# Unread products in TensorE's waits and one operation for a token selection's one-hots, in a diffusion layer with expert choice

## The chip, the cores and the metric

The kernel runs on one core of one Trainium2 chip. The metric is the device time of one execution in microseconds, taken as the median over several runs. The engines are TensorE (PE in the profile; its weight loads are listed apart as PEld), VectorE (DVE), ScalarE (ACT), GpSimd (POOL) and SyncE (SP), which here only issues DMAs.

## The reference

One layer of a diffusion backbone on 1024 latent tokens of 1024 features and 256 context tokens: a mixer (differential attention and a gated linear recurrence side by side, one output projection), and then a mixture of experts in which each expert chooses its tokens. The change touches the second part and the way into it:

```python
def expert_choice_ffn(h, w_router, w_gate, w_up, w_down):
    b_, t_, d_ = h.shape
    cap = CAPACITY_FACTOR * t_ // N_EXPERTS        # 2 * 1024 // 16 = 128
    aff = softmax(einsum("btd,de->bte", h, w_router))
    top_aff, top_idx = top_k(swapaxes(aff, 1, 2), cap)
    xin = h[top_idx]                               # 128 tokens for each expert
    g = einsum("becd,edf->becf", xin, w_gate)
    u = einsum("becd,edf->becf", xin, w_up)
    y = einsum("becf,efd->becd", silu(g) * u, w_down) * top_aff
    return zeros.at[top_idx].add(y)
```

Sixteen experts each take the 128 tokens with the highest affinity to them, run a gated feed-forward of width 1024 on these, and add the weighted result to the tokens' rows.

## The kernel before

**Router tail (lines 1338 to 1363).** The last tiles of the output projection are followed by the router's three steps for tiles 5, 6 and 7: `route_a` (norm and transposition), `route_b` (affinities), `route_c` (the stream that is gathered later, stored to DRAM as `h2d`). This is one chain over DVE, GpSimd (a power), ACT and PE.

**Search (lines 1422 to 1453).** The 128th highest affinity of each of the 16 experts is found by bits in ten rounds, for all experts at once. A round adds seven steps to the best value so far (`cand`, L1442), compares all affinities with the candidates in two halves (`reach`, shown as T, L1447), counts over the tokens with eight products against a matrix of ones (`tot`, L1450), and keeps the highest candidate that at least 128 tokens reach (`best`, L1452 and L1453). Between the products and `best` a generator, `spare()`, gives DVE one operation of other work in some rounds. In round 4 pools change and the next weights are asked for.

**Slots (L1457 to L1470).** From the thresholds each token gets its slot 1 to 128 in each expert's list, by sums over tokens: 24 small products into `sl_ps`.

**A token selection, `pick(e)` (L1477) and `gather(e)` (L1486).** For each of the eight tiles of 128 tokens DVE compares an iota row with the tile's slots (L1482), which gives a 128x128 one-hot matrix, and PE multiplies it, as the stationary operand, with a table of five columns (`aux`: affinity in three parts and two parts of the token's number) into `ix` (L1483). `gather` copies that (L1491), makes the index (L1492), and starts an indirect DMA of 128 rows into `xg` (L1498). The rows are transposed in two groups of four (`tr`, L1504), and split in a high part (`xhi`, ACT, L1505) and a low part (`xlo`, DVE, L1506).

**The experts (L1516 to L1664).** Every weight comes in pieces of 512 KB, 24 for an expert, through a ring of `AHEAD` = 37 places that SyncE's queue fills. A piece is split in a high part (`mhi`, ACT, L1380) and a low part (`mlo`, DVE, L1381), three buffers of each, and each product of the reference is three of PE's: high by high, high by low, low by high (L1525 to L1527 for gate and up, L1614 to L1616 for down).

**What sets the order.** Up to L1644 PE, DVE and ACT work in the order that is written. Behind it, until the last expert, the framework's scheduler sets the order of each engine; it may also put work from behind that line ahead of what is written in front of it. DMAs on SyncE's queue go in order.

```python
    pick(0)
    gather(0)
    for i in range(LEAD):
        make()
    pick(1)
    ms.__exit__(None, None, None)
    tk_st.close()
    x_T(0, 0)
    x_T(0, 1)
    gather(1)
```

Of the kernel before, what the change touches and what calls it, by code (L numbers as in the profile page):

```python
# [32 lines left out]
def shape_constants():  # L33
    """Tables that depend on shapes alone."""
    c = {}
    c["k_ident"] = np.eye(128, dtype=np.float32)
    i = np.arange(64)
    m = [((i[:, None] // (2 * h) == i[None, :] // (2 * h)) & (i[:, None] // h != i[None, :] // h)) for h in LEVELS[:-1]]
    c["k_masks"] = np.tile(np.stack(m, 1).astype(np.float32).reshape(64, -1), (2, 1))
    i = np.arange(128)  # L40
    half = 32
    inv = (1.0 / (np.float32(10000.0) ** (np.arange(0, half, 2, dtype=np.float32) / np.float32(half)))).astype(np.float32)
    t = np.arange(T)
    ang_r = ((t // 64).astype(np.float32)[:, None] * inv).astype(np.float32)
    ang_c = ((t % 64).astype(np.float32)[:, None] * inv).astype(np.float32)
    ang = np.concatenate([ang_r, ang_r, ang_c, ang_c], -1)
    sign = np.where((np.arange(64) % 32) < 16, -1.0, 1.0).astype(np.float32)
    c["k_cos"] = np.ascontiguousarray(np.tile(np.cos(ang).T, (2, 1)))
    c["k_sin"] = np.ascontiguousarray(np.tile((np.sin(ang) * sign).T, (2, 1)))
    c["k_tri"] = (i[:, None] <= i[None, :]).astype(np.float32)  # L50
    c["k_iota"] = np.tile(np.arange(1, 129, dtype=np.float32), (128, 1))
    c["k_pos"] = np.stack([np.tile(np.arange(8, dtype=np.float32), (128, 1)),
                           np.tile(i[:, None].astype(np.float32), (1, 8))], -1).reshape(128, 16)
    step = np.arange(1, 8)[None, :] << np.arange(12, -1, -3)[:, None]
    c["k_step"] = np.tile(step.reshape(-1).astype(np.float32), (128, 1))
    return c


def weave(main, back):
    """Emit two lists of steps in proportion, the second filling in between the steps of the first."""  # L60
    n, m = len(main), len(back)
    j = 0
    for i, f in enumerate(main):
        f()
        while j < m and (j + 1) * n <= (i + 1) * m:
            back[j]()
            j += 1
    while j < m:
        back[j]()
        j += 1  # L70
# [3 lines left out]
def layer(ctx: ExitStack, tc, a, out):  # L74
# [28 lines left out]
    def rstd_of(dst, ss, n, w):  # L103
        """dst = (ss / n + eps) ** -0.5 on [128, w]"""
        nc.vector.tensor_scalar(dst, ss, 1.0 / n, EPS, op0=OP.mult, op1=OP.add)
        nc.gpsimd.tensor_tensor(dst, dst, half_neg[:, :w], op=OP.pow)
# [4 lines left out]
    def cut(halves, ts, hs=slice(None)):  # L111
        """heads hs, tokens ts of a transposed output kept in two halves of the tokens"""
        b, t0 = divmod(ts.start, 512)
        return halves[b][:, hs, t0:t0 + ts.stop - ts.start]
# [44 lines left out]
    def unit_T(job, ppool, t0, n):  # L159
        """transposed output [cols, tokens t0..t0+n]"""  # L160
        def f():
            pp = ppool.tile([128, 512], F32, name="pp", bufs=2)
            for k in range(KT):
                whi, wlo = job.piece(job.hi, k), job.piece(job.lo, k)
                hh, hl = h_hi[t0 // 512][:, k, :], h_lo[t0 // 512][:, k, :]
                nc.tensor.matmul(pp[:, :n], whi, hh, start=(k == 0), stop=False)  # L166
                nc.tensor.matmul(pp[:, :n], whi, hl, start=False, stop=False)  # L167
                nc.tensor.matmul(pp[:, :n], wlo, hh, start=False, stop=(k == KT - 1))  # L168
            job.evac(pp, t0, n)
        return f  # L170

    def unit_N(job, ppool, t, halves=False):
        """natural output, two token tiles t, t + 1, 256 columns"""
# [96 lines left out]
    def hgrn_steps(h):  # L270
# [23 lines left out]
        def blocks(lhs, rhs):  # L294
            """the products of 64 x 64 blocks, half z of tile t on the partitions from 64 z"""
# [231 lines left out]
    # shift and scale: each of their four blocks of 512 columns has its own columns of the array  # L527
# [22 lines left out]
    def small_vectors():  # L550
        nc.vector.tensor_copy(masks.rearrange("p l s -> p (l s)"), mf[:, :masks.shape[1] * 64])
        # small vectors as columns
# [76 lines left out]
    def trans_pair(p):  # L629
        """token tiles 2p, 2p + 1 transposed"""  # L630
# [7 lines left out]
    def mod_pair(p):  # L638
        """modulated, split"""
# [48 lines left out]
    for h in range(4):  # L688
        if h < 3:
            weave(phases[h + 1], hgrn_steps(h))  # L690
        else:
            # the gates multiply finished heads only: head 3's gate waits for its recurrence
# [34 lines left out]
    # the rest of adaLN: rows of gate 1, shift 2, scale 2, gate 2  # L727
# [62 lines left out]
    def prep_first():  # L790
        """the scaled queries and the keys of head 0 as hi and lo, stacked along the contraction for each map"""
# [24 lines left out]
    def prep_steps(h):  # L816
        """the same for a later head, in steps: (for the scalar engine, for the vector engine and the queue)"""
# [152 lines left out]
    def early_weights():  # L970
        """the keys and queries are all stacked: their place goes to the first weights of the output projection"""
# [35 lines left out]
    def mm_y(y, oh, ol, k, n):  # L1007
        """one product of the output projection; oh, ol: the block of k of the activations"""
# [17 lines left out]
    def split_da(hs):  # L1026
        """heads hs of the first two tiles of tokens"""
# [12 lines left out]
    def rest_weights():  # L1040
        """in the order of the places of the raw weights: those of oyd come free first"""
# [17 lines left out]
    # router on the normed stream: the modulation goes into its weights and into a bias  # L1059
# [118 lines left out]
    # A piece is 128 rows of each partition's share: of the gate or of the projection up (half of the columns, two  # L1178
    # blocks of the contraction) or of the projection down (one block).
    AHEAD, LEAD, MAN = 37, 2, 1  # L1180
# [5 lines left out]
    def ring():  # L1186
        """the next place of the ring"""
# [37 lines left out]
    def prep(i):  # L1225
        """the residual, and the activations of the output projection as hi and lo"""
# [52 lines left out]
    def route_b(i, tag="o"):  # L1279
        """the affinities; each fourth of the contraction on its own columns of the array, the fourths then summed"""  # L1280
# [26 lines left out]
    def route_c(i, n=None, queue=nc.sync):  # L1307
        """the modulated stream, to be gathered; in two steps"""
# [46 lines left out]
    next(close7)  # L1355
    next(route6)
    run(route_b(5))
    next(close7)
    run(route_b(6, "atr"))
    run(route_c(6))  # L1360
    run(route_a(7, True))
    run(route_b(7))
    rw, rw_st = pool("rw", side="right")

# [11 lines left out]
    def split_piece(u):  # L1376
        """a fetched piece as hi and lo"""
# [13 lines left out]
    def spare():  # L1391
        """what the vector engine does while the tensor engine counts"""
# [19 lines left out]
    # The 128th highest value of each expert, three bits of it at a time: first the upper 15 of its 30 bits, then  # L1412
    # the lower ones, with every value that the upper ones put above (below) at the upper (lower) end. In 16 bits.
# [6 lines left out]
    for r in range(10):  # L1420
        if r == 4:
# [4 lines left out]
            # what the first expert needs lies where the last tile of tokens is still at work, the ring above it  # L1426
# [22 lines left out]
        for i in range(8):  # L1449
            nc.tensor.matmul(tot, onesb, reach[:, :, i, :], start=(i == 0), stop=(i == 7))  # L1450
        next(todo, None)
        nc.vector.scalar_tensor_tensor(b0[:, 1:8, :], tot, CAP - 0.5, cand, op0=OP.is_ge, op1=OP.mult)  # L1452
        nc.vector.tensor_reduce(b1[:, 0, :], b0.rearrange("p j e -> p e j"), axis=AX.X, op=OP.max)  # L1453
    # slots 1..128 in token order, higher values before those equal to the 128th
# [20 lines left out]
    mops, mops_st = pool("mops", space=PSUM)  # L1475

    def pick(e):  # L1477
        x = ex[e]
        ix = mops.tile([128, 8], F32, name="ix")
        for i in range(8):  # L1480
            oh = mo.tile([128, 128], BF, name="onehot", bufs=3)
            nc.vector.tensor_scalar(oh, iota, slot[:, 0, i, e:e + 1], None, op0=OP.is_equal)  # L1482
            nc.tensor.matmul(ix[:, 0:5], oh, aux[:, i, e, :], start=(i == 0), stop=(i == 7))  # L1483
        x.ix = ix

# [55 lines left out]
    # Every row is closed with what the experts before the last gave it; then the rows of the last one anew.  # L1541
# [90 lines left out]
    def take(u):  # L1632
        """a piece of the weights; the pieces after it are split ahead of their use"""
# [5 lines left out]
    pick(0)  # L1639
    gather(0)  # L1640
    for i in range(LEAD):
        make()
    pick(1)
# [5 lines left out]
    for e in range(NE):  # L1649
        if e == NE - MAN:  # L1650
            ms = tc.manual_schedule(engines={nc.tensor.engine, nc.vector.engine, nc.scalar.engine, nc.gpsimd.engine})
            ms.__enter__()
        gate_up(e, 0)
        if e + 2 < NE:
            pick(e + 2)
# [43 lines left out]
```

## Time and profile before

| | |
|---|---|
| median of 3 runs | 1558.53 us (1556.73 to 1561.23) |
| span of the profiled execution | 1557.5 us |
| its median-to-span difference | 1.0 us |
| PE busy | 1447.3 us (93%) |
| PEld busy | 1191.3 us (76%) |
| DVE busy | 1166.5 us (75%) |
| ACT busy | 875.7 us (56%) |
| POOL busy | 115.4 us (7%) |

An engine's busy time is the sum of its instructions without overlap; PEld runs beside PE. In the span's chain of waits PE stands for 37% and no other engine for more than 2%, the rest being in shorter steps. A time in the rows below is in us from the start of the span. What follows is read from stretches of the span, since the shares over the whole mix stages with different limits: the router tail, the search and the first selection lie between 886 and 976 us, the later experts behind it.

### The profile page before, as it was taken

The page shows a single profiled execution, that of the slowest core. Times are in us where ns is not written, and L with a number is a line of the kernel's source. Part 1 is how long each engine was busy: PE and PEld are TensorE (multiplying, and loading weights), DVE is VectorE, ACT ScalarE, POOL GpSimd, SP SyncE. Part 2 cuts the span into 40 slices and gives each one's busy share as a digit, 9 for nine tenths or more (in the row PEclk, how much of TensorE's full clock was granted, in tenths as well). Part 3 has the DMA queues.
Part 4 walks back from the last instruction along what each step waited for, and adds up shares of the span by engine and source line. Part 5 has one row for each costly group of instructions (what it writes and reads, how often), then busy time and mean ns, then how long its engine had stood idle before and what let it go on. Part 6 is the DMA issues. An engine that isn't in the chain of part 4 may idle for free. (4 is left out here: it accounts for less than half of the span.)

```text
span 1557.5 us, 23415 instructions
## 1 busy us (share of the span) xinstructions
PE 1447.3 (93%) x8808; PEld 1191.3 (76%) x8808; DVE 1166.5 (75%) x1700; ACT 875.7 (56%) x1350; POOL 115.4 (7%) x139
## 2 busy tenths in 40 slices
PE   6999999999999988999999839999999999999990
PEld 1888988888977777999878627777777777777770
DVE  2627472849177769999845578999999999999983
ACT  1734443444211127889843406787777787877781
POOL 1100000000000001110000000110000000000003
PEclk9899999999999998999999859999999999999995
DMA  9210110011166526434056887999999999999736
GB/s 335 82 54 29 28 28 28 29 41 29 30 194 180 177 56 156 96 84 134 15 173 219 303 292 267 365 373 383 365 376 385 378 384 384 367 383 380 270 122 148
DMA packets 159309, 316.28 MB, mean 203 GB/s; under 512 B 13790, under 2 KB 50870, under 8 KB 159196
## 3 DMA queue, kind: packets, MB, share of 16 engines
q1 hardware_dynamic: 148592, 277.99, 50.0%
q0 software_dynamic: 9408, 33.54, 9.1%
q10 hardware_dynamic: 1196, 3.26, 0.6%
q8 instruction: 69, 1.13, 0.3%
q14 instruction: 44, 0.36, 0.1%
HBM read 274.36 MB, written 29.38 MB: 195 GB/s over the span
## 5 line engine op out<-in xcount | busy, mean ns | idle before, releaser
L1381 DVE TENSOR_TENSOR mlo<-mraw,mhi 128x1024 fp32r<-128x1024 f32 x340 | 406.0, 1220 | 25.0 <-ACT mhi L1380 22.1
L1380 ACT CAST mhi<-mraw 128x1024 fp32r<-128x1024 f32 x340 | 354.9, 1051 | 100.2 <-PE g L1526 44.3
L166 PE MATMUL pp<-h_hi,whi 128*128 128x512 f32 (+1 forms) x480 | 180.1, 375 | 0.0
L167 PE MATMUL pp<-h_lo,whi 128*128 128x512 f32 (+1 forms) x480 | 178.4, 372 | 0.0
L168 PE MATMUL pp<-h_hi,wlo 128*128 128x512 f32 (+1 forms) x480 | 178.1, 371 | 0.0
L150 ACT CAST whi<-wraw 128x512 fp32r<-128x512 f32 x64 | 39.6, 621 | 121.5 <-PE pp L167 59.6
L1525 PE MATMUL g<-mhi,xhi 128*128 128x512 f32 x256 | 106.5, 416 | 0.7 <-ACT xhi L1505 0.7
L1614 PE MATMUL my<-mhi,hhi 128*128 128x512 f32 x256 | 104.3, 407 | 0.0
L881 DVE TENSOR_REDUCE sm<-s 128x1 f32<-128x1280 f32 x64 | 95.2, 1490 | 12.0 <-PE s L876 9.6
L166 PEld LDWEIGHTS pp<-h_hi,whi 128*128 128x128 f32 x480 | 90.5, 189 | 17.6 <-ACT T L478 0.9
L168 PEld LDWEIGHTS pp<-h_hi,wlo 128*128 128x128 f32 x480 | 90.5, 188 | 17.0 <-issue 1.7
L1527 PE MATMUL g<-mlo,xhi 128*128 128x512 f32 x256 | 103.1, 403 | 0.2
L1616 PE MATMUL my<-mlo,hhi 128*128 128x512 f32 x256 | 103.1, 403 | 0.1
L1526 PE MATMUL u<-mhi,xlo 128*128 128x512 f32 x256 | 102.5, 400 | 0.0
L167 PEld LDWEIGHTS pp<-h_lo,whi 128*128 128x128 f32 x480 | 90.5, 189 | 15.6 <-issue 0.9
L1527 PE MATMUL u<-mlo,xhi 128*128 128x512 f32 x256 | 102.2, 399 | 0.0
L1615 PE MATMUL my<-mhi,hlo 128*128 128x512 f32 x256 | 101.6, 397 | 0.0
L1525 PE MATMUL u<-mhi,xhi 128*128 128x512 f32 x256 | 101.5, 396 | 0.0
L1526 PE MATMUL g<-mhi,xlo 128*128 128x512 f32 x256 | 101.3, 396 | 0.0
L185 PE MATMUL pp<-whi,h_hi 128*128 128x256 f32 x320 | 93.3, 291 | 2.0 <-ACT h_hi L651 2.0
L343 DVE TENSOR_TENSOR X<-X,T 128x640 f32<-128x640 f32 (+1 forms) x112 | 78.2, 759 | 20.4 <-ACT KM L321 12.8
L186 PE MATMUL pp<-whi,h_lo 128*128 128x256 f32 x320 | 92.1, 288 | 0.7 <-DVE h_lo L652 0.7
(323 smaller groups left out, 3135.3 us busy)
## 6 DMA issues: line engine op xcount, KB each, us to landing
mraw<-in_w_gate_dram SPq DMA_DIRECT2D x114, 512.0 KB
mraw<-in_w_up_dram SPq DMA_DIRECT2D x113, 512.0 KB
mraw<-in_w_down_dram SPq DMA_DIRECT2D x113, 512.0 KB
wraw<-in_w_in_dram SPq DMA_DIRECT2D x32, 512.0 KB
aw<-in_w_ada_dram SPq DMA_DIRECT2D x64, 256.0 KB
aw<-in_w_ada_dram SPq DMA_DIRECT2D x16, 512.0 KB
T<-in_w_up_dram SPq DMA_DIRECT2D x15, 512.0 KB
T<-in_w_down_dram SPq DMA_DIRECT2D x15, 512.0 KB
```

The costliest lines, as they stand in the source:

```text
L166: nc.tensor.matmul(pp[:, :n], whi, hh, start=(k == 0), stop=False)
L167: nc.tensor.matmul(pp[:, :n], whi, hl, start=False, stop=False)
L168: nc.tensor.matmul(pp[:, :n], wlo, hh, start=False, stop=(k == KT - 1))
L881: nc.vector.tensor_reduce(self.sm[:, m:m + 1], s, axis=AX.X, op=OP.max, negate=True)
L1380: nc.scalar.copy(hi, r)
L1381: nc.vector.tensor_sub(lo, r, hi)
L1525: nc.tensor.matmul(o, x.hi[:, k, :], hi[:, kk, :], start=(k == 0), stop=False)
L1526: nc.tensor.matmul(o, x.lo[:, k, :], hi[:, kk, :], start=False, stop=False)
L1527: nc.tensor.matmul(o, x.hi[:, k, :], lo[:, kk, :], start=False, stop=(k == 7))
L1614: nc.tensor.matmul(y[:, ns], x.hh[:, k, :], hi[:, ns], start=(k == 0), stop=False)
L1615: nc.tensor.matmul(y[:, ns], x.hl[:, k, :], hi[:, ns], start=False, stop=False)
L1616: nc.tensor.matmul(y[:, ns], x.hh[:, k, :], lo[:, ns], start=False, stop=(k == 7))
```

## The change

`keep_on(o, n)` is new: it issues n bf16 products of 128x128 by 128x512, of the matrix of ones with itself repeated, into a part of PSUM that nothing reads. They are put between the steps of the router tail (3, 4, 3 and 3, and 9 behind it), behind the counting products of each round (5, and 8 in round 4), behind the first `gather` (8) and behind the second `pick` (14): 97 in all. `pick` makes its eight one-hots with one DVE operation over 128x1024 into one buffer (before: eight operations, three buffers), and returns a function that issues the eight products, which for the later experts is called between the two halves of the gate and up projection. The ring has 36 places instead of 37. The rest of the diff takes comments out.

```diff
-    AHEAD, LEAD, MAN = 37, 2, 1
+    AHEAD, LEAD, MAN = 36, 2, 1
...
+    def keep_on(o, n):
+
+        for _ in range(n):
+            nc.tensor.matmul(o, onesb, onesb[:, None, :].to_broadcast([128, 4, 128]), start=True, stop=True)
+    idle = atps.tile([128, TA], F32, name="s1")[:, 0:512]
     next(route6)
     run(route_b(5))
+    keep_on(idle, 3)
     next(close7)
     run(route_b(6, "atr"))
     run(route_c(6))
-    run(route_a(7, True))
-    run(route_b(7))
+    keep_on(idle, 4)
+    route7 = route_a(7, True)
+    next(route7)
+    keep_on(idle, 3)
+    next(route7)
+    rb = route_b(7)
+    next(rb)
+    keep_on(idle, 3)
+    run(rb)
+    keep_on(idle, 9)
...
             nc.tensor.matmul(tot, onesb, reach[:, :, i, :], start=(i == 0), stop=(i == 7))
+        keep_on(idle, 8 if r == 4 else 5)
         next(todo, None)
...
         ix = mops.tile([128, 8], F32, name="ix")
-        for i in range(8):
-            oh = mo.tile([128, 128], BF, name="onehot", bufs=3)
-            nc.vector.tensor_scalar(oh, iota, slot[:, 0, i, e:e + 1], None, op0=OP.is_equal)
-            nc.tensor.matmul(ix[:, 0:5], oh, aux[:, i, e, :], start=(i == 0), stop=(i == 7))
+        oh = mo.tile([128, 8, 128], BF, name="onehot")
+        nc.vector.tensor_tensor(oh, iota[:, None, :].to_broadcast([128, 8, 128]),
+                                slot[:, 0, :, e:e + 1].to_broadcast([128, 8, 128]), op=OP.is_equal)
+
+        def counts():
+            for i in range(8):
+                nc.tensor.matmul(ix[:, 0:5], oh[:, i, :], aux[:, i, e, :], start=(i == 0), stop=(i == 7))
         x.ix = ix
+        return counts
...
-    pick(0)
+    pick(0)()
     gather(0)
+    idle = mops.tile([128, 512], F32, name="g", bufs=2)
+    keep_on(idle, 8)
     for i in range(LEAD):
         make()
-    pick(1)
+    pick(1)()
+    keep_on(idle, 14)
     ms.__exit__(None, None, None)
...
+        counts = pick(e + 2) if e + 2 < NE else None
         gate_up(e, 0)
-        if e + 2 < NE:
-            pick(e + 2)
+        if counts:
+            counts()
         gate_up(e, 1, lambda: hid_T(e, 0))
```

In the changed kernel lines 1380 and 1381 become 1395 and 1396, 1450 becomes 1465, 1482 and 1483 become 1497 and 1502, 1491 becomes 1511, 1504 to 1506 become 1524 to 1526, 1525 to 1527 become 1545 to 1547, and 1614 to 1616 become 1634 to 1636.

The order moves in three places. On PE, between the selection of expert 0 and the first expert (`ix` from the one-hots is a selection's product, `tr` a transposition of the gathered rows, `g` and `u` the sums of gate and up, and in the changed kernel also where the unread products go), the rows before are:

```order
L1483 MATMUL ix<-aux,onehot 128x5
L1504 MATMUL tr<-ident,xg 128x128
L1483 LDWEIGHTS onehot
L1483 MATMUL ix<-aux,onehot 128x5
L1504 MATMUL tr<-ident,xg 128x128
L1483 LDWEIGHTS onehot
L1483 MATMUL ix<-aux,onehot 128x5
L1504 MATMUL tr<-ident,xg 128x128 x2
L1525 MATMUL g<-mhi,xhi 128x512
L1525 MATMUL u<-mhi,xhi 128x512
L1504 MATMUL tr<-ident,xg 128x128 x4
L1526 MATMUL g<-mhi,xlo 128x512
```

and now, with eight unread products in a row where the first of them stands, eight selection products where the next one stands, and fourteen unread ones behind these:

```order
L1502 MATMUL ix<-aux,onehot 128x5
L1360 LDWEIGHTS onesb
L1360 MATMUL g<-onesb 128x512
...
L1524 MATMUL tr<-ident,xg 128x128 x2
L1502 LDWEIGHTS onehot
L1502 MATMUL ix<-aux,onehot 128x5
...
L1360 LDWEIGHTS onesb
L1360 MATMUL g<-onesb 128x512
...
L1524 MATMUL tr<-ident,xg 128x128 x2
```

Sixteen selection products (experts 0 and 1) stand ahead of the first transposition before; now eight do, and between the first two transpositions and the next two come the eight products of expert 1 and fourteen unread ones.

On DVE, from the splits of the first weights to the first `xlo`, the rows before are:

```order
L1381 TENSOR_TENSOR mlo<-T,mhi 128x1024 x2
L1482 TENSOR_SCALAR onehot<-k_iota_c,slot 128x128 x8
L1381 TENSOR_TENSOR mlo<-T,mhi 128x1024
L1506 TENSOR_TENSOR xlo<-tr,xhi 128x512
L1491 COPY ax<-ix 128x5
L1482 TENSOR_SCALAR onehot<-k_iota_c,slot 128x128
```

and now:

```order
L1396 TENSOR_TENSOR mlo<-T,mhi 128x1024 x2
L1497 TENSOR_TENSOR onehot<-k_iota_c,slot 128x1024
L1396 TENSOR_TENSOR mlo<-T,mhi 128x1024
L1511 COPY ax<-ix 128x5
L1497 TENSOR_TENSOR onehot<-k_iota_c,slot 128x1024
...
L1511 COPY ax<-ix 128x5
L1497 TENSOR_TENSOR onehot<-k_iota_c,slot 128x1024
L1526 TENSOR_TENSOR xlo<-tr,xhi 128x512
```

Ahead of the first `xlo` stood the one-hots of experts 0 and 1; now those of experts 2 and 3 stand there too, each behind the copy of an earlier expert's `ix`.

On PE in the gate and up projection of a later expert, the products of a selection stood by ones and twos between the others:

```order
L1525 MATMUL u<-mhi,xhi 128x512
L1483 LDWEIGHTS onehot
L1483 MATMUL ix<-aux,onehot 128x5
L1526 MATMUL u<-mhi,xlo 128x512
L1527 MATMUL u<-mlo,xhi 128x512
L1525 MATMUL u<-mhi,xhi 128x512
L1526 MATMUL u<-mhi,xlo 128x512
L1483 LDWEIGHTS onehot
L1483 MATMUL ix<-aux,onehot 128x5
L1527 MATMUL u<-mlo,xhi 128x512
```

and now all eight stand in the projection down (`my`), ahead of the transpositions of the next expert's rows:

```order
L1634 MATMUL my<-mhi,hhi 128x512
L1502 LDWEIGHTS onehot
L1502 MATMUL ix<-aux,onehot 128x5
...
L1502 LDWEIGHTS onehot
L1502 MATMUL ix<-aux,onehot 128x5
L1524 MATMUL tr<-ident,xg 128x128 x4
L1635 MATMUL my<-mhi,hlo 128x512
```

A selection's products have moved from five places to one.

## Rows read from the trace of the kernel before

**Rows 1.** Windows: us, busy of PE, PEld, DVE, ACT, POOL, granted clock, DMA.

```profile
876.00:886.80 10.80, 8.93 (x73) 7.21 (x75) 4.96 (x11) 5.71 (x13) 0.94 (x2) 1.00 0.99 321
886.80:896.30 9.50, 4.99 (x41) 2.97 (x32) 6.96 (x24) 3.70 (x12) 1.22 (x3) 0.50 1.03 410
896.30:921.50 25.20, 9.07 (x80) 7.57 (x81) 21.61 (x67) 2.94 (x3) 0.00 (x0) 0.50 0.92 309
...
933.90:941.40 7.50, 6.78 (x21) 5.14 (x22) 2.70 (x10) 2.22 (x3) 0.96 (x1) 0.50 0.41 137
...
976.10:1481.60 505.50, 505.38 (x2343) 396.83 (x2341) 480.96 (x605) 399.56 (x435) 39.13 (x27) 1.00 1.01 367
```

**Rows 2.** Timeline, router tail: start, duration, engine, line, operation, [idle before and releaser].

```profile
894.52 0.23 DVE L1293 SCALAR_TENSOR_TENSOR L<-lg,st,rbias 128x16 f32<-128x16 f32 x1 [0.66 <-POOL st L106]
...
897.07 0.93 PE L1450 MATMUL tot<-T,onesb 128*128 128x112 bf16 x8 [3.55 <-DVE T L1447]
```

**Rows 3.** Timeline, rounds of the search.

```profile
902.10 0.74 DVE L1312 SCALAR_TENSOR_TENSOR h<-x,st,a 128x512 f32<-128x512 f32 x1
...
902.88 0.27 DVE L1452 SCALAR_TENSOR_TENSOR best<-tot,cand 128x112 uint16<-128x112 f32 x1
...
907.72 0.27 DVE L1452 SCALAR_TENSOR_TENSOR best<-tot,cand 128x112 uint16<-128x112 f32 x1 [0.30 <-PE tot L1450]
...
919.36 0.69 DVE L1447 TENSOR_TENSOR T<-low,cand 128x448 bf16<-128x448 uint16 x2
919.80 0.91 PE L1450 MATMUL tot<-T,onesb 128*128 128x112 bf16 x8 [1.51 <-DVE T L1447]
...
920.75 0.27 DVE L1452 SCALAR_TENSOR_TENSOR best<-tot,cand 128x112 uint16<-128x112 f32 x1 [0.69 <-PE tot L1450]
```

**Rows 4.** Timeline, slot sum.

```profile
923.79 0.42 DVE L1469 TENSOR_TENSOR slot<-sl_ps,T 128x256 f32<-128x256 f32 x1 [1.96 <-PE sl_ps L1466]
```

**Rows 5.** Timeline, selection of expert 0 to its first products.

```profile
924.57 0.96 DVE L1482 TENSOR_SCALAR onehot<-k_iota_c,slot 128x128 bf16<-128x128 bf16 x5
...
926.57 0.17 DVE L1491 COPY ax<-ix 128x5 f32<-128x5 f32 x1 [0.28 <-PE ix L1483]
...
933.95 0.47 PE L1504 MATMUL tr<-ident,xg 128*128 128x128 f32 x1 [3.21 <-DMA xg<-h2d,idx]
...
935.93 0.69 DVE L1506 TENSOR_TENSOR xlo<-tr,xhi 128x512 fp32r<-128x512 f32 x1 [3.92 <-ACT xhi L1505]
...
937.68 0.78 PE L1526 MATMUL g<-mhi,xlo 128*128 128x512 f32 x1
...
941.24 0.47 PE L1526 MATMUL u<-mhi,xlo 128*128 128x512 f32 x1
```

**Rows 6.** Timeline of an expert, then groups by line (count, busy, mean ns, idle).

```profile
986.07 0.39 PE L1527 MATMUL u<-mlo,xhi 128*128 128x512 f32 x1
986.31 0.23 PE L1483 MATMUL ix<-aux,onehot 128*128 128x5 bf16 x3
...
986.72 0.39 PE L1526 MATMUL g<-mhi,xlo 128*128 128x512 f32 x1
...
987.87 0.40 PE L1525 MATMUL u<-mhi,xhi 128*128 128x512 f32 x1
988.11 0.18 PE L1483 MATMUL ix<-aux,onehot 128*128 128x5 bf16 x1
...
988.46 0.40 PE L1527 MATMUL u<-mlo,xhi 128*128 128x512 f32 x1
...
L1483 PEld LDWEIGHTS <-onehot 128*128 128x128 bf16 x104 | 7.0, 97 | 14.6 <-DVE onehot L1482 7.1 <-issue 6.6
...
L1381 DVE TENSOR_TENSOR mlo<-mraw,mhi 128x1024 fp32r<-128x1024 f32 x340 | 406.0, 1220 | 25.0 <-ACT mhi L1380 22.1
```

**Rows 7.** Waits in the experts: engine, line, releaser: us, times, longest.

```profile
ACT mhi L1380 <- PE g L1526: 47.2, 86, 1.4
...
ACT mhi L1380 <- DMA mraw<-in_w_up_dram: 1.0, 2, 0.6
```

## Prediction

> **What bounds the kernel now.** I began with the windows [rows 1]. They cut the time from the router's tail to the end of the experts into stretches, and two things are to be seen there. From 886.8 to 941.4 us the granted clock of TensorE (PE) is 0.50, the lower of its two levels, 1.2 GHz; before it and in the experts it is 1.00, 2.4 GHz. The fall came after PE had begun to wait for the router's chain, and the rise after PE had again been at work for 7 us (6.78 of 7.5 us busy). And from 976 to 1481.6, fourteen experts, PE is busy without a gap (505.38 of 505.50), while VectorE (DVE) is busy for 480.96, or 95%. So there are two regimes: a serial front of 55 us, where PE is one link of a chain, and an expert phase that PE alone sets.
>
> Then the timeline of the front. In the tail the last affinities (L1293 at 894.52) waited for GpSimd's power, not for PE, and PE then idles 3.55 us before the first count [rows 2]. In a round of the search the chain is candidates, comparison, eight counting products, threshold. A spare DVE operation stands behind the products: in rounds one to four it ends 0.04 us before the threshold starts (902.10 + 0.74 against 902.88), so PE is not what is waited for there; in the last round, without one, DVE waits 0.69 us for PE [rows 3]. Such a wait of 0.3 us or more stands in four of ten rounds, the first of them at 907.72. Next comes the slot sum, 1.96 us of DVE waiting for PE [rows 4], then the pick of expert 0, the gather (7.38 us from 926.57 to the first transposition at 933.95), and the first products, which run 0.43 us apart until 941.24 [rows 5]; in the expert phase such products stand 0.23 us apart [rows 6].
>
> **The change part by part.** The 97 unread products have 512 columns each; the nearest rows are the float32 products of 512 columns, so I take 0.23 us each at the high level and 0.43 at the low one.
>
> Tail, 22 of them: 13 stand between links of the chain. Between 886.8 and 896.3 PE is busy 4.99 of 9.5 us, and 4.5 us of room hold 13 x 0.23 = 3.0, or at the low level not quite 5.6. What is waited for last is GpSimd, 0.66 us. The nine behind fit the 3.55 us idle (2.1, at the low level 3.9). I take 0, with ends of -0.3 (faster links) and +2.
>
> Rounds: five products behind the counts take 1.15 us and have 1.51 (the wait in front of the next counts). So at the high level they cost nothing. What the level gives is smaller than the 0.91 us of the counts suggests. The second four of the eight wait for the second half of the comparison, so only 4 x 112 columns shorten, by 0.19 us, and in six rounds the spare operation ends last. I take 0.2 us in four rounds, 0.05 in six: -1.0. If the level is low, five cost 2.15, which is 0.64 us over the room, in each round.
>
> Slot sum: its products stream 2176 columns in all, 1.81 us at 1.2 GHz and 0.91 at 2.4: -0.9. Pick of expert 0: now 2.00 us (924.57 to 926.57). The one operation over 128x1024 takes two operands of unequal width, so I price it as the subtraction of the same size, 1.22 us (lower end 0.8, at the pace of the 16-bit comparison, 0.69 for twice 448); with eight products behind it about 2.0 at either price of PE: 0. Up to the gather that is -1.9.
>
> The first expert is where the order decides. The eight fillers and the pick of expert 1 were written ahead of the transpositions, but the program order puts the first two transpositions of xg, which wait for the gather, between them. So PE runs eight fillers (1.9 us), then idles for some 5 us, and everything else comes after the landing: pick 1, 14 fillers, two transpositions, pick 2, and on DVE the one-hots of pick 3 ahead of xlo. The fillers thus do not fill the gather's wait; 14 of them stand on the path, and begin at the low level, as the first products do now. Worked out from the landing: two transpositions and eight index products 0.85 (0.47, and eight starts 0.05 apart); fillers 5.2, if the level rises some 5 us after work resumes (ten at 0.43, four at 0.23); two transpositions and pick 2, 0.65, at the high level; copy 0.17; one-hots 1.22; xlo 0.69; four transpositions 0.45: 9.2 us to the product L1526. Now that is 3.73 us (937.68), followed by eight products in 3.56 us that would take 1.84 at the high level, so it corresponds to 5.45. The step costs +3.7; with all fillers at the high level +1.8; with all at the low one, and the eight products too, +6.3.
>
> Expert phase. An index product between weight products costs more than itself [rows 6]. From 986.07 to 986.72 two steps of 0.23 have three of them between and take 0.65, so the three cost 0.19; from 987.87 to 988.46 two steps have one between and take 0.59, so the one costs 0.13. A first one thus costs 0.12 to 0.13 and each further one 0.03. Before, a pick's eight stand in five groups (three, one, one, two, one): with 0.12 and 0.027, which the rounding of the rows allows, 0.18 + 3 x 0.12 + 0.15 = 0.69 us. Together they cost 0.12 + 7 x 0.027 = 0.31. Fourteen picks lie in this phase before; after, picks 2 and 3 have moved ahead of it: 14 x 0.69 - 12 x 0.31 = 5.9 us less of PE's time, and PE is the bound. DVE gets one operation of 1.22 for eight that take 0.19 each (0.96 for five, [rows 5]). Whether it keeps up is the open point: one piece of work of 1.22 us can make a lower half (mlo) late. ScalarE's waits for PE (47.2 us on L1526 alone) against 1.0 for the weights of the up projection say that PE's release of buffers paces the loop, not the fetches [rows 7]. I take -5.9; ends 0 and -6.3 (with 0.13 and 0.03). For the same reason the ring of 36 places for 37 costs nothing: what covers it is the lead of the fetches over their use; without that cover a place is worth one piece, 1.5 us (505.5 us for 14 experts of 24 pieces).
>
> Sum: -1.9 + 3.7 - 5.9 = -4.1 on a span of 1557.5, so 1553.4. The runs' median, 1558.5, is 1.0 above the span, and I forecast 1554.3.
>
> **The weight load, weighed.** The loads of the one-hots as weights last 97 ns each [rows 6], but three index products take 0.23 us and one takes 0.18, so loads that stand together overlap. If they did not, eight together would cost 8 x 0.097 + 0.09 = 0.87 us, more than the scattered 0.69. The Trainium skill, TensorE: Matmul & The Clock Gate, section LDWEIGHTS (loading the stationary operand), gives a load as its columns over 1.2 GHz, 107 ns for 128; by that a pick would cost about 0.95. The trace's durations agree with the page and its starts do not.
>
> **Rivals.**
> 1. The level rises early, or the first expert's fillers meet the high level: -1.9 + 1.8 - 5.9 = -6.0, 1552.5. For it: 14 dense products come right where now there are gaps. Against: PE idles some 5 us ahead of them, and in the front the level fell while PE was busier than that.
> 2. The picks free nothing, since DVE, at 95%, delivers the lower halves later by what PE gains: -1.9 + 3.7 = +1.8, 1560.3. For it: the one piece of 1.22. Against: less DVE time in all, and ScalarE waits for PE.
> 3. The weight loads of eight products together do not overlap: 12 x 0.87 - 9.7 = +0.7 in the expert phase, in all +2.5, 1561.0. Against it the three starts above.
> 4. Slower: the level is low through the search, and the fillers become the round's longest link: 10 x 0.64 = +6.4 in the rounds, +0.3 behind the tail, +6.3 in the first expert, -5.9: +7.1, 1565.6. For it: the level fell at 886.8, and the first fillers come hardly before that. Against: at the low level they make PE busy almost throughout, and in [rows 1] the level rose after such a stretch. It decides from six low rounds on (0.3 + 6.3 - 5.9 + 6 x 0.64 = 4.5).
> That the change does not do what it says is in the forecast: in the gather's wait there are 1.9 us of fillers and the rest stands behind it.
>
> **Chances and numbers.** Forecast 0.58 (its own range 1551.8 to 1557); rivals 0.16, 0.14, 0.04, 0.08. About 0.3%, 4.7 us, is what a measurement can tell from no change. Faster by more means under 1553.8: 0.4 of the forecast and nearly all of rival 1, 0.39. Slower by more, over 1563.2: most of rival 4, 0.08. The rest is 0.53. The range goes from 1550.3 (rival 1 with the ends of the tail and the fillers) to 1561.0 (rivals 2 and 3).
>
> **What would show it.** Granted clock 1.00 from the tail through the rounds, with rounds of about 2.2 us (2.42 now, half of 902.88 to 907.72); the slot sum's wait near 1.0; the clock at 0.50 when xg lands, and 14 products of line 1360 between its first two transpositions and the next two; 9 us from landing to L1526's successor, line 1546; experts 35.8 us apart instead of 36.1. I am wrong if the fillers run before the landing, if experts stay at 36.1, or if the counts in the rounds start late because PE still streams fillers.

## The result, and the profile after

The changed kernel takes 1550.43 us (median of 4 runs, 1549.72 to 1550.48), against 1557.7 for the kernel before with four runs (1556.73 to 1561.23): a ratio of 0.9949, with a 95% interval of 0.9936 to 0.9962. Timed again on another chip, where before took 1559.51, it took 1549.76: 0.9940 (0.9928 to 0.9952). The forecast was 1554.3, a gain of 4.2 us, and "no change that can be measured" was its likeliest case (0.53). The gain is 7.3 us, and 9.75 on the other chip, at or just past the lower end of the stated range (1550.3): the forecast was wrong.

The windows of the changed kernel, with the columns of [rows 1], two stretches more:

```profile
886.80:896.30 9.50, 7.64 (x65) 3.64 (x63) 6.99 (x24) 3.63 (x12) 1.11 (x3) 1.00 1.02 404
896.30:921.50 25.20, 19.17 (x157) 10.56 (x157) 21.92 (x70) 2.94 (x3) 0.00 (x0) 1.00 0.88 311
921.50:926.60 5.10, 3.42 (x16) 1.15 (x16) 4.55 (x9) 0.00 (x0) 1.47 (x1) 0.69 0.64 213
926.60:933.90 7.30, 2.72 (x15) 1.39 (x16) 3.40 (x7) 0.00 (x0) 0.00 (x0) 0.73 0.77 281
933.90:941.40 7.50, 6.51 (x38) 3.55 (x37) 3.33 (x9) 1.17 (x2) 0.38 (x1) 0.79 0.00 0
...
976.10:1481.60 505.50, 505.36 (x2367) 408.54 (x2366) 485.99 (x513) 412.19 (x442) 53.17 (x28) 1.00 1.01 370
```

The level stays at 1.00 through tail and search, where it was 0.50, and falls in the selection of expert 0 and the gather. In the expert phase PE is as busy as before, but the same 505.5 us hold records of 24 more products.

Three stretches show where the 9.7 us of span went (1557.5 to 1547.8; the two profiled executions lie further apart than the medians, which differ by 7.3). They are cut at the first count, the copy of expert 0's `ix`, and the first product of the projection down of expert 0 and of expert 15. In the kernel before these stand at 897.07, 926.57, 962.77 and 1504.84; the changed kernel's are in this timeline:

```profile
896.96 0.66 PE L1465 MATMUL tot<-T,onesb 128*128 128x112 bf16 x8 [2.05 <-DVE T L1462]
...
918.55 0.28 DVE L1468 SCALAR_TENSOR_TENSOR best<-tot,cand 128x112 uint16<-128x112 f32 x1 [0.45 <-PE tot L1465]
...
920.77 0.42 DVE L1485 TENSOR_TENSOR slot<-sl_ps,T 128x256 f32<-128x256 f32 x1 [1.13 <-PE sl_ps L1482]
...
923.23 0.17 DVE L1511 COPY ax<-ix 128x5 f32<-128x5 f32 x1 [0.45 <-PE ix L1502]
...
963.19 0.48 PE L1634 MATMUL my<-mhi,hhi 128*128 128x512 f32 x1
...
1495.53 0.39 PE L1634 MATMUL my<-mhi,hhi 128*128 128x512 f32 x1
```

| kernel | first count to copy | copy to first down | to the last expert's down | median us |
|---|---|---|---|---|
| before | 29.50 | 36.20 | 542.07 | 1557.7 |
| changed | 26.27 | 39.96 | 532.34 | 1550.43 |
| e1, selection's change alone | 29.19 | 35.50 | 533.35 | 1549.53 |
| e2, unread products alone | 26.60 | 37.25 | 540.86 | 1558.59 |
| e3, 36 in the gather | 26.30 | 33.03 | 532.77 | 1546.29 |
| e4, eight small one-hots | 26.29 | 37.26 | 532.65 | 1549.81 |
| e5, before with 8 places | 29.20 | 35.52 | 534.16 | 1552.08 |
| e6, without the 14 | 26.29 | 35.26 | 533.44 | 1546.96 |
| e7, 36 in the gather alone | 29.21 | 35.14 | 532.77 | 1549.72 |
| e8, before with ring of 36 | 29.51 | 36.09 | 542.12 | 1560.75 |
| e9, 33 in the gather | 26.30 | 33.99 | 532.63 | 1545.89 |
| e10, changed again | 26.28 | 39.07 | 532.42 | 1549.76 |

The kernel before, run beside them, had medians of 1559.86 (e1 to e4), 1560.03 (e5 to e8) and 1559.51 (e9, e10); so a time is best read by its ratio to that. Against before, the front gives 3.2 us, the first expert takes 3.8, and the experts give 9.7; 0.5 us lie outside the three stretches. The stretches come from one execution each and the medians from all: the profiled runs of e2 and e7 are 3.1 and 2.7 us below their medians, and that of e10 is 2.2 above. The first count itself stands anywhere from 895.6 to 900.9 us in these twelve profiles, 2.6 us apart for the changed kernel and e10, which are the same code; so it is the stretches that can be compared, not the spans.

The first expert in the changed kernel, PE's timeline from the selection of expert 0 to the first product with `xlo`:

```profile
922.84 0.35 PE L1502 MATMUL ix<-aux,onehot 128*128 128x5 bf16 x8 [2.10 <-DVE onehot L1497]
923.05 3.21 PE L1360 MATMUL g<-onesb 128*128 128x512 bf16 x8
931.18 0.66 PE L1524 MATMUL tr<-ident,xg 128*128 128x128 f32 x2 [4.92 <-DMA xg<-h2d,idx]
931.64 0.40 PE L1502 MATMUL ix<-aux,onehot 128*128 128x5 bf16 x8
931.90 5.74 PE L1360 MATMUL g<-onesb 128*128 128x512 bf16 x14
937.47 0.38 PE L1524 MATMUL tr<-ident,xg 128*128 128x128 f32 x2
...
940.50 0.48 PE L1546 MATMUL g<-mhi,xlo 128*128 128x512 f32 x1
```

PE idles 4.92 us for the landing, then fourteen unread products run for 5.74 in front of the other transpositions; from the landing to L1546 it is 9.32 us.

An expert of the changed kernel, PE in the projection down: a group of four transpositions alone, and one with the eight products of a selection ahead of it.

```profile
1002.31 0.39 PE L1634 MATMUL my<-mhi,hhi 128*128 128x512 f32 x1
1002.54 0.60 PE L1524 MATMUL tr<-ident,T 128*128 128x128 f32 x4
1002.90 0.48 PE L1635 MATMUL my<-mhi,hlo 128*128 128x512 f32 x1
...
1004.84 0.39 PE L1634 MATMUL my<-mhi,hhi 128*128 128x512 f32 x1
1005.07 0.35 PE L1502 MATMUL ix<-aux,onehot 128*128 128x5 bf16 x8
1005.29 0.64 PE L1524 MATMUL tr<-ident,xg 128*128 128x128 f32 x4
1005.68 0.48 PE L1635 MATMUL my<-mhi,hlo 128*128 128x512 f32 x1
```

From product to product the first takes 0.59 us (1002.31 to 1002.90) and the second 0.84 (1004.84 to 1005.68), so eight products together cost 0.25 us of PE.

And what the prediction didn't read, in the kernel before. PE in the projection down of one expert, then DVE beside it:

```profile
1002.20 0.48 PE L1614 MATMUL my<-mhi,hhi 128*128 128x512 f32 x1
1002.52 0.39 PE L1615 MATMUL my<-mhi,hlo 128*128 128x512 f32 x1
1002.86 0.50 PE L1616 MATMUL my<-mlo,hhi 128*128 128x512 f32 x1
1003.21 0.40 PE L1614 MATMUL my<-mhi,hhi 128*128 128x512 f32 x1
...
1000.39 0.69 DVE L1506 TENSOR_TENSOR xlo<-tr,xhi 128x512 fp32r<-128x512 f32 x1
1001.00 0.68 DVE L1531 SCALAR_TENSOR_TENSOR T<-T,u 128x512 f32<-128x512 f32 x1
1001.59 2.35 DVE L1381 TENSOR_TENSOR mlo<-mraw,mhi 128x1024 fp32r<-128x1024 f32 x2
```

and a row of the waits in the expert phase (us in total, times, longest):

```profile
PEld my L1616 <- DVE mlo L1381: 5.7, 15, 0.4
```

Two steps of 0.34 and 0.35 stand where others take 0.23. The first of the two lower halves that DVE begins at 1001.59 is what L1616 waits for; DVE is busy without a gap up to it, with `xlo` and the product with `u` (L1531) just ahead. This comes back in each expert but the last: 15 waits, 0.4 us each for the load, and two steps of PE that are 0.2 us longer in all. The waits of the weight loads in the changed kernel hold no such row:

```profile
PEld L1502 <- issue: 3.3, 12, 0.3
PEld g L1547 <- DVE mlo L1396: 1.1, 2, 0.6
PEld tr L1524 <- DVE hlo L1526: 0.6, 2, 0.3
```

### The profile page after: what moved, and what is told of

The parts are those of the page before. It is cut to its first block, busy times and chain, and to the rows that moved or that the text cites. A ratio compares the mean times of both kernels' runs of the same rounds, so it can differ in the third digit from the quotient of the medians.

```text
span 1547.8 us, 23432 instructions
## 1 busy us (share of the span) xinstructions
PE 1451.9 (94%) x8905; PEld 1198.4 (77%) x8905; DVE 1165.9 (75%) x1588; ACT 880.5 (57%) x1350; POOL 128.8 (8%) x139
## 5 line engine op out<-in xcount | busy, mean ns | idle before, releaser
L881 DVE TENSOR_REDUCE sm<-s 128x1 f32<-128x1280 f32 x64 | 95.3, 1491 | 14.2 <-PE s L876 11.8
L1545 PE MATMUL g<-mhi,xhi 128*128 128x512 f32 x256 | 102.3, 399 | 0.5 <-ACT xhi L1525 0.5
L1546 PE MATMUL g<-mhi,xlo 128*128 128x512 f32 x256 | 101.1, 395 | 0.0
L1546 PE MATMUL u<-mhi,xlo 128*128 128x512 f32 x256 | 100.7, 393 | 0.0
```

The lines of the kernel that those rows point to most:

```text
L881: nc.vector.tensor_reduce(self.sm[:, m:m + 1], s, axis=AX.X, op=OP.max, negate=True)
L1545: nc.tensor.matmul(o, x.hi[:, k, :], hi[:, kk, :], start=(k == 0), stop=False)
L1546: nc.tensor.matmul(o, x.lo[:, k, :], hi[:, kk, :], start=False, stop=False)
```

## The experiments

**e1: the selection's change alone.** All `keep_on` calls are taken out.

```diff
-    keep_on(idle, 3)
...
-        keep_on(idle, 8 if r == 4 else 5)
...
-    keep_on(idle, 14)
```

> The selection's change alone (one operation for the one-hots, its eight products together, ring of 36), without any unread product. Theory A (the parts add): the expert phase keeps the whole gain of the changed kernel, 35.5 us from one projection down to the next instead of 36.2, -9.7 us; the front stays at the low level up to the gather, as before, apart from 0.3 us in selection 0; the first expert costs 0.6 more than before (eight products of selections 1 and 2 among its transpositions). Sum -9.4: 1548.3, faster than the changed kernel. Theory B (the unread products help the experts too, by an earlier start of the loop or an earlier fetch): experts at 35.8 or more, 1552 to 1554.

1549.53 us, a ratio of 0.9935 (0.9918 to 0.9951), that is, no slower than the whole change. The experts keep 8.7 of the 9.7 us, and the interval between two projections down is 35.49 to 35.54 while selections last. So most of the experts' gain owes nothing to the unread products, as theory A had it. Of the missing 1.0 us, 0.9 lies in the last three intervals (35.51, 35.74 and 35.90, for 35.31, 35.34 and 35.60 in the changed kernel); why was not isolated.

**e2: the unread products alone.**

```diff
-        oh = mo.tile([128, 8, 128], BF, name="onehot")
+        for i in range(8):
+            oh = mo.tile([128, 128], BF, name="onehot", bufs=3)
...
-        if counts:
-            counts()
+        if e + 2 < NE:
+            pick(e + 2)
```

> The 97 unread products alone, with the selection as before (eight one-hots, products scattered, ring of 37). Theory A: granted clock 1.00 through the search, the copy of ix 3.0 us earlier; fourteen products on the path behind the landing, +3.8; experts at 36.2 as before. Sum +0.8: 1558.5. Theory B: experts at 35.9 or less, 1554 or less.

1558.59, a ratio of 0.9992 (0.9982 to 1.0002): no change. In the profiled run, the fastest of the ten, the search gains 2.9 and the first expert loses 1.05, not 3.8. Of these 2.7 us, 0.6 is the gather: the rows land 7.34 us behind the copy, and 7.95 in the changed kernel. Another 1.45 is the level, which was back earlier behind the landing (0.77 from 926.6 to 933.9, and 1.00 from 933.9 to 941.4, against 0.73 and 0.79 in the changed kernel): the fourteen take 4.12 us to the next transposition instead of 5.57. Here six of selection 1's products follow the eight unread ones ahead of the landing, as in the kernel before, where 14 of the 16 selection products stood ahead of the first transposition and not all 16. From the third interval on the experts are at 36.2, and the row of late lower halves is there again:

```profile
PEld my L1632 <- DVE mlo L1396: 4.6, 12, 0.4
```

**e4: eight small one-hots, products together.** One operation, or one place?

```diff
-        nc.vector.tensor_tensor(oh, iota[:, None, :].to_broadcast([128, 8, 128]),
-                                slot[:, 0, :, e:e + 1].to_broadcast([128, 8, 128]), op=OP.is_equal)
+        for i in range(8):
+            nc.vector.tensor_scalar(oh[:, i, :], iota, slot[:, 0, i, e:e + 1], None, op0=OP.is_equal)
```

> The changed kernel with the one-hots made by eight small operations into the one buffer; the products still follow together. If the gain in the experts comes from the products' place (TensorE's steps): experts at 35.5, 1550.4 to 1551. If it comes in part from VectorE's single operation, the wait of the low halves in the projection down returns (two steps of 0.34 for 0.23 in each expert): experts at 35.7, +2.7, 1553.

1549.81, 0.9941 (0.9922 to 0.9959), with experts at 35.5 and one wait of 0.2 us for the lower halves in the projection down. VectorE's single operation is not what gives the gain.

**e5: the kernel before with eight places for the one-hots.** This is the smallest edit that should give the gain, if the place is what matters.

```diff
-    AHEAD, LEAD, MAN = 37, 2, 1
+    AHEAD, LEAD, MAN = 36, 2, 1
...
-            oh = mo.tile([128, 128], BF, name="onehot", bufs=3)
+            oh = mo.tile([128, 128], BF, name="onehot", bufs=8)
```

> The kernel before with eight places for the one-hots instead of three (and a ring of 36); still eight small operations, the products issued in the same loop, no unread product. In the order the products of a later expert's selection then stand in two groups (two to four ahead of a group of transpositions, the rest together in the next gate projection) instead of five. Theory A (the scheduler's place for the products is set by how many one-hots may wait, and that place is the gain): experts at 35.6, without the two steps of 0.34 us per expert; 7.5 less than before, some 1551.5. Rival (the gain needs the one operation on VectorE or the products written apart): experts at 36.2, 1559.

1552.08, 0.9941 (0.9924 to 0.9957), with experts at 35.52 to 35.63. Its products stand in two groups, as in this timeline:

```profile
1005.50 0.20 PE L1483 MATMUL ix<-aux,onehot 128*128 128x5 bf16 x2
1005.56 0.64 PE L1504 MATMUL tr<-ident,xg 128*128 128x128 f32 x4
...
1022.56 0.30 PE L1483 MATMUL ix<-aux,onehot 128*128 128x5 bf16 x6
1022.73 0.48 PE L1525 MATMUL g<-mhi,xhi 128*128 128x512 f32 x1
```

and the late lower halves are down to one:

```profile
PEld my L1616 <- DVE mlo L1381: 0.4, 1, 0.4
```

So one number, three places or eight, holds most of what the changed code gives to the experts (7.9 of 9.7 us; e8 shows that the ring's 36 places have no part in it). With three places a fourth one-hot has to wait for the first product. That this is why the scheduler spreads the products over the projections is my reading of the order, not shown by itself.

**e8: the ring of 36 alone.**

```diff
-    AHEAD, LEAD, MAN = 37, 2, 1
+    AHEAD, LEAD, MAN = 36, 2, 1
```

> The kernel before with a ring of 36 places instead of 37, nothing else. Theory A (the fetches' lead covers it): experts at 36.2, no change, within 1 us of before. Rival (a place is worth a piece): +1.5, and waits of ScalarE for the weights' transfers in the expert phase.

1560.75, 1.0006 (0.9996 to 1.0015): nothing, and ScalarE's longest wait is the same as before, for PE:

```profile
ACT mhi L1380 <- PE g L1526: 47.2, 86, 1.4
```

**e6: without the fourteen.**

```diff
     pick(1)()
-    keep_on(idle, 14)
```

> The changed kernel without the fourteen unread products behind the second selection. Theory A (they stand on the path behind the landing and return only a part by an earlier rise of the level): from the copy of ix to the first projection down 36.5 to 37.5 us instead of 39.96, 1547 to 1548. Rival (they pay for themselves by the level): 39.5 or more, 1550 or more.

1546.96, 0.9915 (0.9898 to 0.9931). The first expert takes 35.26 us from the copy, 4.7 less than in the changed kernel (0.5 of it because the rows land 7.46 us behind the copy and not 7.95). Its products with `xlo` and those behind them run at the low level for 2.3 us (934.02 to 936.29), and yet the first comes 3.79 us behind the landing, not 9.32:

```profile
930.23 0.66 PE L1524 MATMUL tr<-ident,xg 128*128 128x128 f32 x2 [4.06 <-DMA xg<-h2d,idx]
...
934.02 0.78 PE L1546 MATMUL g<-mhi,xlo 128*128 128x512 f32 x1
```

So the fourteen are a loss where the order puts them.

**e3: 36 in the gather's wait instead.**

```diff
-    keep_on(idle, 8)
+    keep_on(idle, 36)
...
-    keep_on(idle, 14)
```

> The changed kernel with 36 unread products behind the first gather and none behind the second selection; on TensorE all 36 and the products of selection 1 then stand ahead of the first transposition. Theory A (what the first expert lost is the wait ahead of the fourteen and the fourteen themselves): the 36 last 36 x 0.22 = 7.9 us, as long as the gather; the level is high at the landing, and the first expert runs from landing to its projection down in about 26 us (28.8 before, 32.0 in the changed kernel): -6 against the changed kernel, 1544.4. Rival: the level falls in the selection of expert 0 all the same, as in the changed kernel (0.69 from 921.5 to 926.6); then 36 take up to 15.4 us, 7.5 longer than the gather, and the time is 1551 or more.

1546.29, 0.9910 (0.9894 to 0.9927). The level is 1.00 from the search through to the experts, and the first transposition stands right behind the fillers and selection 1:

```profile
927.04 7.93 PE L1360 MATMUL g<-onesb 128*128 128x512 bf16 x36
934.81 0.34 PE L1502 MATMUL ix<-aux,onehot 128*128 128x5 bf16 x8
935.01 0.63 PE L1524 MATMUL tr<-ident,xg 128*128 128x128 f32 x4
...
937.56 0.48 PE L1546 MATMUL g<-mhi,xlo 128*128 128x512 f32 x1
```

From the copy to the first projection down it is 33.03 us (36.20 before); theory A's mechanism held, with 1.9 us less than it promised.

**e7: 36 in the gather and none in tail and search.**

```diff
-    keep_on(idle, 9)
...
-        keep_on(idle, 8 if r == 4 else 5)
...
-    keep_on(idle, 8)
+    keep_on(idle, 36)
```

> The selection's change and 36 unread products behind the first gather, none in the router tail and none in the search. Theory A (terms add): the search and slot sum are 2.9 us longer than with products in the rounds; the 36 begin at the low level and last 8 to 12 us against a gather of 7.4, so 0 to 4 us late, and the first expert then runs at the high level in about 26 us from the first transposition. Sum against the kernel with both (1546.3): +3 to +7, 1549 to 1553. Rival (the rounds' products give nothing that the 36 don't): 1546.5.

1549.72, 0.9934 (0.9917 to 0.9950). The search is 2.9 us longer, and the 36 begin at the low level and last 10.05 us, so the first transposition stands 9.90 us behind the copy, 7.79 in e3 (35.14 to the first projection down against 33.03). By the stretches 5.0 us more than e3, by the medians 3.4, inside theory A's 3 to 7.

**e9 and e10: 33 in the gather, beside the changed kernel.**

```diff
-    keep_on(idle, 8)
+    keep_on(idle, 33)
...
-    keep_on(idle, 14)
```

> The changed kernel with 33 unread products behind the first gather (36 before this, of which the last ended 0.2 us ahead of the first transposition) and none behind the second selection. Theory A (36 ended after the rows had landed): 33 end 0.65 us earlier, the gather's wait is 7.3 to 7.5 instead of 7.8, the level stays at 1.00 to the first expert, and the time is 1545.9, some 4.4 under the changed kernel on the same chip. Rival (the rows land only then): the wait stays 7.8 and the time at 1546.3; or the level falls in the gap, and it is 1547 or more.

> The changed kernel itself, beside the version with 33 products on the same chip. Theory A: 1550 to 1551, first expert from the copy of ix to the first projection down about 39.5 to 40 us, with the level at 0.50 at the landing. If the moment at which the level rises differs from run to run, that stretch can be as short as 37.3, as with eight small one-hots.

e9 has 1545.89, 0.9908 (0.9896 to 0.9921), the best median, and e10 1549.76 on the same chip, 3.9 more. Between 33 and 36 nothing can be told. In the profiled run the level of e9 had fallen in the selection, so its 33 took 8.90 us, longer than 36 did in e3:

```profile
925.43 8.90 PE L1360 MATMUL g<-onesb 128*128 128x512 bf16 x33
934.17 0.34 PE L1502 MATMUL ix<-aux,onehot 128*128 128x5 bf16 x8
```

So e9's theory A (a wait of 7.3 to 7.5) failed in that run: it is 8.76 from the copy. That the median still came to its 1545.9 doesn't bear it out.

e10's first expert took 39.07 us (39.96 in the first profile of the same kernel), and 0.62 of the 0.89 between them is the landing, 7.33 us behind the copy for 7.95; the level at the landing had fallen, as e10's theory A has it (0.85 from 926.6 to 933.9, 0.69 from 933.9 to 941.4).

## Why the prediction was wrong

**The expert phase: -5.9 forecast, -9.7 measured.** This is the step that failed. Its first half held: a scattered selection costs 0.69 us [rows 6] and one together was put at 0.31; it is 0.25. But the sum then took these products for all that PE loses in an expert. An expert went from 36.17 to 35.51 us, 0.66: 0.69 - 0.25 = 0.44 from the products, and the other 0.22 is what the two long steps add ((0.34 + 0.35) - 2 x 0.23 = 0.23) for a lower half that came late once in each expert. The sum had nothing for that. The profile had it as 15 waits of L1616, and I read only ScalarE's waits beside it, which say that DVE isn't the bound on average. That average, 95%, hid one place where it is late each time. Over the fifteen intervals 0.22 is 3.3 us, most of the 3.8 that were missed. The new place of the selection's products took this away too: the wait is left once in e1, e4, e5 and e6, in the last interval, and comes 12 and 15 times in e2 and e8, where the products are spread; e5 and e8 differ in the number of places alone.

How it does so stays open. DVE's order around the wait is not enough: expert 13 of the kernel before has no selection left beside it (the last product of one is at 1425.3), and DVE does there what it does in the changed kernel (a lower half, the product with `u`, `xlo`, two lower halves):

```profile
1433.38 1.23 DVE L1381 TENSOR_TENSOR mlo<-mraw,mhi 128x1024 fp32r<-128x1024 f32 x1 [0.25 <-PE tr L1504]
1434.53 0.68 DVE L1531 SCALAR_TENSOR_TENSOR T<-T,u 128x512 f32<-128x512 f32 x1
1435.12 0.68 DVE L1506 TENSOR_TENSOR xlo<-tr,xhi 128x512 fp32r<-128x512 f32 x1
1435.72 2.35 DVE L1381 TENSOR_TENSOR mlo<-mraw,mhi 128x1024 fp32r<-128x1024 f32 x2
...
1436.99 0.19 PEld L1616 LDWEIGHTS my<-mlo,hhi 128*128 128x128 f32 x1 [0.38 <-DVE mlo L1381]
```

and the load is late by the same 0.38 us. The last two intervals, which have no selection, are 0.8 us shorter in all, and this wait is in both of them before and in neither now; the rest of that, some 0.3 us, is within what they differ by among all versions (0.5 and 0.3 us).

**DVE as the bound (rival 2): no.** The phase shrank, and DVE was busy for 5 us more in the same window (485.99 for 480.96), with more of the experts' work in it.

**The rounds: -1.0 forecast.** From the first count to the last threshold it was 23.68 us ([rows 2, 3], 897.07 to 920.75) and is 21.59 (896.96 to 918.55). (0.2 us in four rounds and 0.05 in six make 1.1, not 1.0; that changes nothing here.) I had taken a threshold that starts 0.04 us after the spare operation's end as one that waited for nothing. The changed kernel shows what not waiting looks like:

```profile
901.66 0.75 DVE L1312 SCALAR_TENSOR_TENSOR h<-x,st,a 128x512 f32<-128x512 f32 x1
...
902.32 0.27 DVE L1468 SCALAR_TENSOR_TENSOR best<-tot,cand 128x112 uint16<-128x112 f32 x1
```

A free operation starts 0.09 us ahead of the recorded end of the one before (901.66 + 0.75 - 902.32). So in this round, too, PE had been late, by 0.13 us. The rounds' lengths say the same: before, from threshold to threshold it was 2.41 to 2.43 us in each but the one with the pool change, with a spare operation or without. Now the six rounds that were put at 0.05 are shorter by 0.12 to 0.25 each, 1.1 in all, and the four put at 0.2 by 0.23 to 0.27, 1.0 in all.

**Slot sum and selection of expert 0: -0.9 and 0 forecast.** The slot sum fell from 3.04 us (920.75 to 923.79) to 2.22 (918.55 to 920.77): -0.8, right. The selection fell from 2.78 (923.79 to 926.57) to 2.46 (920.77 to 923.23): -0.3, since the one operation cost 1.22, as priced, and less stood behind it.

**The first expert: +3.7 forecast, +3.8 measured, by the path described, and in part by luck.** The landing found the level at 0.73 on average, the fourteen ran at the low level but for the last, and from the landing to L1546 it was 9.3 us (9.2 forecast). e6 and e3 confirm it from the other side. But the landing came 7.95 us behind the copy (7.38 before), 0.57 that the sum doesn't have, and the way from L1546 to the first projection down was 0.7 us shorter than the sum allowed (22.69; before 25.09, less 3.56 - 1.84); the two cancel. e10, the same kernel, took 0.9 us less in this stretch than the first profile, most of it by an earlier landing.

**The other rivals.** Rival 1 gave nearly the time, but by another way: its fillers at the high level didn't come about. Rival 3 (loads that don't overlap, 0.87 us) falls with 0.25, and so does the 0.95 that I worked out from the Trainium skill, TensorE: Matmul & The Clock Gate, section LDWEIGHTS (loading the stationary operand): loads that last 96 to 97 ns (107 by that section) overlap here, eight products in 0.22 us (1005.07 to 1005.29). Rival 4 (low level in the search) is out: 1.00. The ring costs nothing (e8), as forecast.

## What to carry to other kernels

A buffer count can set the order: where a scheduler places work, see first what a producer with few buffers forces it to interleave, since here eight places for three did most of what a rewritten selection did. On an engine that is the bound, list each step of one period that is longer than its neighbours, before pricing the change; a wait that comes once in a period is worth what it adds to that period, times the periods, whatever the average says of the engine it waits for. Filler work belongs ahead of the wait in the order that the engine really has; behind the landing it is on the path.

## What the runs showed of the hardware that was not expected

Eight weight loads of 128x128 in bf16, each followed by a product of five columns, took 0.22 us together at the high level, 27 ns for each pair, though the profile gives 96 ns to a load. The comparison over 128x1024 with a bf16 result took as long (1.22 us) as a float32 subtraction of that size. And the records of DVE's operations overlap by up to 0.09 us (901.66 + 0.75 against 902.32), so an idle time of zero there may hide a wait. The gather of the same 128 rows took 7.17 (e8) to 7.95 us (the changed kernel) from the copy of `ix` to the first transposition, in the nine profiles in which PE stood idle until it landed.
